# Fifty of 256 gathered dot products move to the matmul engine, and routing is cut into pieces

## The chip, the core and the metric

The kernel runs on one core of a Trainium2 chip. A core has five engines with instruction streams of their own: TensorE (PE) for matmuls, VectorE (DVE), ScalarE (ACT), GpSimd (POOL) and SyncE (SP), which only starts transfers here. Transfers run on 16 DMA engines. The metric is the device time of one execution in microseconds (us).

## What is computed

Two transformer blocks on 256 tokens of width 2048, all in float32. The change is in the last part of the first block, a layer of 16384 small experts ("PEER"). Cut to what matters:

```python
# peer(x = hn, ...): T = 256 tokens, H = 8 heads, K = 16 picks a head, 128 keys a side
qry = (xt @ w_query).reshape(T, H, 2, 128)
s = einsum('thpd,phnd->thpn', qry, sub_keys)          # 2 x 128 scores per token and head
top_s, top_i = top_k(s, 16)                           # the best 16 of each side
cand_s = top_s[:, :, 0, :, None] + top_s[:, :, 1, None, :]
best_s, best_pos = top_k(cand_s.reshape(T, H, 256), 16)
expert_idx = ...                                      # first key * 128 + second key
gates = softmax(best_s)
u = expert_down[expert_idx]                           # one row of 2048 numbers per pick
act = gelu(einsum('td,thkd->thk', xt, u))             # the dot products
y = einsum('thkd,thk->td', expert_up[expert_idx], gates * act)
```

There are 256 x 8 x 16 picks, so 32768 rows of 8 KB of `expert_down` are read, 268 MB.

## The kernel before

**Row tiles.** Tokens stand in two tiles of 128, one token on each of 128 partitions. For tile t, head hd and pick k, one indirect transfer that POOL starts (`gather`, L612) fetches 128 rows, one for each token: a row tile of 128 x 2048, 1.05 MB. There are 2 x 8 x 16 = 256 of them. They are fetched in pairs into a buffer of 16 KB a partition, from a pool of seven such buffers (`bigt`). The pool also holds `h` and `hn` for all this time, `hhi`/`hlo` and `qT` at the start, and a `cchunk` from tile 1 on. So two buffers serve for rows at first, then five, and four in tile 1. A new pair is fetched into a buffer when both row tiles in it have been used.

**The dot product** of a row tile with the tokens is one DVE instruction (L621): it multiplies by `hn[:, t, :]` and sums over 2048 columns into one column of `dots`. After 16 of them ACT takes the Gelu (L625) and DVE multiplies by the gates (L626).

**Routing** (`route`, L564 to L606) finds the 16 picks of one tile and head on DVE: some 30 small instructions, with one Exp on ACT. `route_to` keeps it a head or two ahead of the rows.

**Coefficients.** The sum over `expert_up` is not done row by row for three quarters of the columns, but as a dense product with a matrix of coefficients. It is built per token as an outer product of two one-hot vectors: the second key's one-hot, and the first key's one-hot times the coefficient (L667), by one matmul of 128x128 for each token (L669). A group is four tokens. `store_coefs` builds it for tile 0 while tile 1's rows are fetched, and writes three of four chunks to DRAM (`ct_d`, 2 MB each). `onehots_ahead` has ACT build second-key one-hots for 112 of tile 1's 128 tokens into buffers that are free. What is left for tile 1 (32 groups) comes after the last row tile. Then the products with `expert_up` begin (L807).

**Order.** A scheduler lays out each engine's stream at build time, and each engine then runs its stream strictly in that order, waiting where a semaphore is not there yet. A step of a background generator (`bg`) is taken once a pair of row tiles.

## Time and profile before

| | us |
|---|---|
| median of 3 runs (3211.7 to 3215.2) | 3213.9 |
| the profiled execution | 3219.45 |
| its span from first to last instruction | 3217.7 |
| first gather of a row tile / first gather of head 1 | 827.11 / 886.72 |
| end of the last row tile's dot product | 1573.9 |
| DVE busy / POOL busy / PE busy, whole span | 2535.2 / 879.8 / 2555.4 |

All times in the trace are microseconds from the start of the span. The heads are counted 0 to 15 over both tiles. The stage of the row tiles is from about 827 to 1574, slices 11 to 20 of the page's 40. [...]

### The profile page before, as it was taken

Reading aid. Unit: us, or ns where it says so; the run is one execution under the profiler, and the core shown is the slowest. Engines: PE = TensorE matmul, PEld = TensorE weight load, DVE = VectorE, ACT = ScalarE, POOL = GpSimd, SP = SyncE. Lnnn points to the kernel's source line nnn. Section 1 sums busy time; section 2 is a strip of 40 time slices with the busy share of each in tenths; the row PEclk is TensorE's granted clock in tenths of the full one; section 3 lists DMA queues with packets and bytes.
Section 4 is the critical chain, followed back from the end, with each engine's and each line's share of the span. In section 5 each row is a group of like instructions: output and inputs, shape, how many; then the busy total and the mean of one; then the engine's idle time right before and its main releaser. Section 6 shows DMA issues by size and latency. Waiting matters only on the chain. (4 is left out here: it accounts for less than half of the span.)

```text
span 3217.7 us, 35193 instructions
## 1 busy us (share of the span) xinstructions
PE 2555.4 (79%) x12368; PEld 2141.8 (67%) x12368; DVE 2535.2 (79%) x3682; ACT 1542.9 (48%) x2212; POOL 879.8 (27%) x575
## 2 busy tenths in 40 slices
PE   8999999999910004400399999999999999999999
PEld 7788888888810003300388888889987787878777
DVE  6656544555999999999988888887575799999974
ACT  5534444444310105441244444457445677778764
POOL 0000000000376686667766666620000000000000
PEclk9999999999965555555699999999999999999999
DMA  6455555565899999999789999974654599999964
GB/s 239 151 182 162 184 191 195 187 220 197 328 352 363 331 427 387 376 342 419 285 306 334 335 334 334 334 263 142 204 190 139 201 338 348 381 344 379 348 226 167
DMA packets 302522, 898.22 MB, mean 279 GB/s; under 512 B 20736, under 2 KB 42240, under 8 KB 268288
## 3 DMA queue, kind: packets, MB, share of 16 engines
q1 hardware_dynamic: 226560, 542.88, 48.1%
q0 software_dynamic: 57760, 335.65, 27.3%
q10 hardware_dynamic: 18016, 17.35, 1.6%
q8 instruction: 99, 1.62, 0.2%
q14 instruction: 87, 0.71, 0.1%
HBM read 887.42 MB, written 8.39 MB: 278 GB/s over the span
## 5 line engine op out<-in xcount | busy, mean ns | idle before, releaser
L254 DVE TENSOR_TENSOR wlo<-raw,whi 128x1024 fp32r<-128x1024 f32 (+1 forms) x538 | 648.5, 1208 | 453.1 <-ACT whi L253 446.9
L253 ACT CAST whi<-raw 128x1024 fp32r<-128x1024 f32 (+1 forms) x538 | 559.5, 1041 | 686.9 <-PE pj L284 255.6
L621 DVE CUSTOM_DVE_ANT_0 row<-row,hn 128x2048 f32<-128x2048 f32 x256 | 579.7, 2291 | 6.1 <-DMA row<-in_peer_expert_down_dram,eidx 5.7
L612 POOL DMA_INDIRECT row<-in_peer_expert_down_dram,eidx x256 | 508.4, 1986 | 265.8 <-DVE dots L621 100.7
L199 POOL TENSOR_TENSOR r<-rstdv,mhalf 128x2 f32<-128x2 f32 x5 | 4.5, 890 | 1508.9 <-DVE rstdv L225 1508.9
L612 POOL DMA_INDIRECT urow<-in_peer_expert_up_dram,eidx x256 | 322.8, 1261 | 197.7 <-DVE h L771 143.8
L254 DVE TENSOR_TENSOR wlo<-rawg,whi 128x1024 fp32r<-128x1024 f32 x256 | 313.1, 1225 | 35.1 <-ACT whi L253 10.3
L253 ACT CAST whi<-rawg 128x1024 fp32r<-128x1024 f32 x256 | 270.0, 1056 | 97.9 <-PE pgu L1283 68.6
L282 PE MATMUL pj<-whi,xhi 128*128 128x512 f32 x736 | 289.4, 393 | 1.3 <-ACT whi L253 1.3
L283 PE MATMUL pj<-wlo,xhi 128*128 128x512 f32 x736 | 288.6, 392 | 0.0
L284 PE MATMUL pj<-whi,xlo 128*128 128x512 f32 x736 | 288.2, 392 | 0.0
L639 PE MATMUL pcf<-cc,pk 128*128 128x128 f32 x2 | 0.9, 460 | 340.7 <-DVE pk L626 340.7
L639 PEld LDWEIGHTS pcf<-cc,pk 128*128 128x128 f32 x2 | 0.4, 182 | 341.5 <-issue 177.8
L1282 PE MATMUL pgu<-wlo,xs 128*128 128x512 f32 x512 | 199.8, 390 | 3.1 <-DVE wlo L254 3.1
L1281 PE MATMUL pgu<-whi,xs 128*128 128x512 f32 x512 | 200.0, 391 | 0.0
L1283 PE MATMUL pgu<-whi,xs 128*128 128x512 f32 x512 | 199.2, 389 | 0.0
L771 DVE SCALAR_TENSOR_TENSOR h<-urow,pk,h 128x512 f32<-128x512 f32 x256 | 191.8, 749 | 4.5
L254 DVE TENSOR_TENSOR wlo<-rawd,whi 128x1024 fp32r<-128x1024 f32 x128 | 154.1, 1224 | 12.1 <-ACT whi L253 1.1
L282 PEld LDWEIGHTS pj<-whi,xhi 128*128 128x128 f32 x736 | 138.5, 188 | 29.5 <-ACT whi L253 1.7
L284 PEld LDWEIGHTS pj<-whi,xlo 128*128 128x128 f32 x736 | 138.4, 188 | 28.1
L283 PEld LDWEIGHTS pj<-wlo,xhi 128*128 128x128 f32 x736 | 138.4, 188 | 27.7
L253 ACT CAST whl<-raw 128x1024 fp32r<-128x1024 f32 x96 | 101.2, 1056 | 113.5 <-PE ua L809 83.0
(547 smaller groups left out, 6302.0 us busy)
## 6 DMA issues: line engine op xcount, KB each, us to landing
raw<-in_w_in_dram SPq DMA_DIRECT2D x124, 1024.0 KB
raw<-in_peer_expert_up_dram SPq DMA_DIRECT2D x96, 1024.0 KB
rawg<-in_w_expert_gate_dram SPq DMA_DIRECT2D x128, 512.0 KB
rawg<-in_w_expert_up_dram SPq DMA_DIRECT2D x128, 512.0 KB
rawd<-in_w_expert_down_dram SPq DMA_DIRECT2D x64, 1024.0 KB
raw<-in_w_out_dram SPq DMA_DIRECT2D x32, 1024.0 KB
raw<-in_w_ret_branch_dram SPq DMA_DIRECT2D x16, 1024.0 KB
raw<-in_w_peer_query_dram SPq DMA_DIRECT2D x16, 1024.0 KB
```

What stands on the lines that cost most here:

```text
L199: G.tensor_tensor(out=dst, in0=v, in1=mhalf[:, 0:n], op=ALU.pow)
L253: S.copy(hi, raw)
L254: env["last"] = V.tensor_tensor(out=lo, in0=raw, in1=hi.bitcast(F32), op=ALU.subtract)
L282: TE.matmul(ps[:, t, :], h_, hi, start=st, stop=False)
L283: TE.matmul(ps[:, t, :], h_, lo, start=False, stop=False)
L284: env["mm"] = TE.matmul(ps[:, t, :], l_, hi, start=False, stop=en)
L612: G.indirect_dma_start(out=dst, out_offset=None, in_=src, in_offset=bass.IndirectOffsetOnAxis(ap=idx, axis=0))
L621: V.tensor_tensor_reduce(out=row[:, i, :], in0=row[:, i, :], in1=hn[:, t, :], scale=1.0, scalar=0.0, op0=ALU.mult, op1=ALU.add, accum_out= ...
L771: V.scalar_tensor_tensor(out=h[:, t, 1536:2048], in0=row[:, k, :], scalar=coef[:, t, c0 + k:c0 + k + 1], in1=h[:, t, 1536:2048], op0=ALU.m ...
L1281: TE.matmul(o_, xh, hi[:, :, i, :], start=k == 0, stop=False)
L1282: TE.matmul(o_, xh, lo[:, :, i, :], start=False, stop=False)
L1283: TE.matmul(o_, xl, hi[:, :, i, :], start=False, stop=k == NK - 1)
```

## The change

**Dots on PE.** `PE_DOTS` names the picks whose dot product goes to PE: picks 1, 4, 7, 10 and 13 in heads 1 to 7, picks 3, 7 and 11 in heads 8 to 12, none in heads 0 and 13 to 15. That is 35 + 15 = 50 of 256. For such a row tile PE makes 16 transposes of 128x128, ACT copies them from PSUM in two halves of 1024 columns, and PE makes 16 float32 matmuls against `hT`, the transposed tokens. The diagonal of the 128x128 result holds the dot products, and one DVE instruction over 128 columns multiplies by the identity and sums. `hT` takes one of the seven large buffers from head 1 to head 12.

**Routing in pieces.** `route` yields eight times, and after each pair of row tiles 1.35 pieces are issued. One multiplication of the gates and one negation leave DVE.

**Coefficients.** In tile 0, two of a group's four first-key one-hots come from ACT. For tile 1, first-key one-hots of 64 tokens are built early into a buffer `o1`, which takes a large buffer from head 13 on. There half of the groups need one DVE instruction of 512 columns instead of three of 128 on DVE and one on POOL.

```diff
+PE_DOTS = [()] + [(1, 4, 7, 10, 13)] * 7 + [(3, 7, 11)] * 5 + [()] * 3
+ROUTE = 1.35
...
+    def transposed_copy(dst, src):
+        for g in range(2):
+            ps = acc("pxT")
+            for j in range(8):
+                TE.transpose(ps[:, j // 4, j % 4 * P:(j % 4 + 1) * P], src[:, (g * 8 + j) * P:(g * 8 + j + 1) * P], ident)
+            S.copy(dst[:, g * 8:g * 8 + 8, :], ps.rearrange("p a (b c) -> p (a b) c", b=4))
...
+    def diagonal(ps, dots, k):
+        junk = env["wk"].tile([P, P], F32, tag="dj", name="dj", bufs=1)
+        V.tensor_tensor_reduce(out=junk, in0=ps[:, 0:P], in1=ident, scale=1.0, scalar=0.0,
+                               op0=ALU.mult, op1=ALU.add, accum_out=dots[:, k:k + 1])
...
-                V.tensor_tensor_reduce(out=row[:, i, :], in0=row[:, i, :], in1=hn[:, t, :], scale=1.0, scalar=0.0,
-                                       op0=ALU.mult, op1=ALU.add, accum_out=dots[:, k + i:k + i + 1])
+                if k + i in on_pe:
+                    rT = rTs[step[1] % 2]
+                    step[1] += 1
+                    transposed_copy(rT, row[:, i, :])
+                    ps = pst("pdd")
+                    for d in range(NK):
+                        TE.matmul(ps[:, 0:P], rT[:, d, :], hT[:, d, t * P:(t + 1) * P], start=d == 0, stop=d == NK - 1)
+                    late.append((step[0] + 2, lambda ps=ps, k=k + i: diagonal(ps, dots, k)))
+                else:
+                    env["dot"] = V.tensor_tensor_reduce(
+                        out=row[:, i, :], in0=row[:, i, :], in1=hn[:, t, :], scale=1.0, scalar=0.0,
+                        op0=ALU.mult, op1=ALU.add, accum_out=dots[:, k + i:k + i + 1])
+            settle(step[0])
+            step[0] += 1
+            with tc.issue_after(env["dot"].ins):
+                route_to(16 + int(ROUTE * step[0]))
             yield
...
+            if not oh:
+                onehots(ab4[:, 1, 2:4], kT, c * 32 + q + 2, 2, 0)
+            first = c * 32 + q
+            ahead = o1[0][:, first // 2:first // 2 + 4] if oh and first % 8 == 0 else None
+            if ahead is not None:
+                V.tensor_tensor(out=ab4[:, 1], in0=ahead, in1=cT[:, first:first + 4, None].to_broadcast([P, 4, P]), op=ALU.mult)
             for i in range(4):
...
+                if not oh and i >= 2:
+                    S.mul(ab4[:, 1, i, :], ab4[:, 1, i, :], cT[:, tk:tk + 1])
...
+            if n == 13:
+                pe_done.append(1)
+                o1.append(bigt([P, 64, P], BF16, "o1"))
+            if n == 1:
+                hT = bigt([P, NK, T], name="hT")
+                for t_ in range(2):
+                    transposed_copy(hT[:, :, t_ * P:(t_ + 1) * P], hn[:, t_, :])
+                rTs = [e8([P, NK, P], name="rT"), raw_tile([P, NK, P], "rT")]
```

How the streams change at two places. First DVE in head 1 (a dot product is the pair of rows `row,dots` and `dots`; MAX to MATCH_REPLACE are routing; `nm` is the negation that leaves). Before:

```order
L621 ISA row,dots<-row,hn 128x2048
L621 ISA dots 128x1
L584 MAX_INDEX bp<-bv,rtmp 128x8
L585 MATCH_REPLACE rtmp<-bv,rtmp 128x256
L602 TENSOR_SCALAR nm<-bv 128x1
```

Now, at the same step of routing (`pdd` is PE's result, `dj` a scratch tile):

```order
L592 MAX_INDEX bp<-bv,rtmp 128x8
L668 ISA row,dots<-row,hn 128x2048
L668 ISA dots 128x1
L594 MATCH_REPLACE rtmp<-bv,rtmp 128x256
L642 ISA dj,dots<-pdd,cc 128x128
L642 ISA dots 128x1
L595 MAX bv<-rtmp 128x8
```

The instruction over `pdd` stands between two dot products of rows, one or two dot products behind the pick that it belongs to; DVE waits there until PE has finished that pick.

Second, PE from the end of the query projection on. Before, nothing stands between the scores and tile 0's coefficients:

```order
L677 MATMUL psr<-skT,qT 128x128 x20
L632 MATMUL pky<-cc,pk 128x128 x2
L639 MATMUL pcf<-cc,pk 128x128
L669 MATMUL pcc<-ab_7357 128x128 x4
L669 MATMUL pcc<-ab_7378 128x128 x4
```

Now the picks of heads 1 to 7 stand there, and those of heads 8 to 12 among the coefficient groups:

```order
L736 MATMUL psr<-skT,qT 128x128 x20
L630 MATMUL pxT<-cc,hn 128x128 x19
L630 MATMUL pxT<-cc,row 128x128 x16
L665 MATMUL pdd<-hT,rT 128x128 x16
```

```order
L728 MATMUL pcc<-ab_8910 128x128 x4
L728 MATMUL pcc<-ab_8944 128x128 x4
L630 MATMUL pxT<-cc,row 128x128 x16
L665 MATMUL pdd<-hT,rT 128x128 x16
L728 MATMUL pcc<-ab_9009 128x128 x4
```

PE takes its picks one after another, transposes and matmuls of each before those of the next. POOL still starts the 256 gathers in the same order, but 16 instead of 32 of its multiplications for tile 1 are left.

## Rows read from the trace of the kernel before

**Rows 1.** The page's slices: TensorE's clock, DVE, DMA.
```profile
span 3217.7 us, 35193 instructions
...
DVE  6656544555999999999988888887575799999974
...
PEclk9999999999965555555699999999999999999999
...
```
**Rows 2.** Busy time by stretch: PE, weight loads, DVE, ACT, POOL, clock, DMA share, GB/s.
```profile
887.00:1100.00 213.00, 13.33 (x92) 12.18 (x90) 210.82 (x469) 28.52 (x60) 141.47 (x72) 0.54 0.93 347
1100.00:1204.00 104.00, 0.00 (x0) 0.00 (x0) 103.40 (x101) 1.53 (x4) 85.36 (x44) 0.50 0.99 411
1204.00:1440.00 236.00, 68.51 (x259) 55.73 (x259) 233.68 (x454) 107.01 (x271) 157.99 (x76) 0.53 0.96 367
1440.00:1574.00 134.00, 0.00 (x0) 0.00 (x0) 125.58 (x116) 22.68 (x69) 98.37 (x51) 0.50 0.98 411
...
1500.00:1550.00 50.00, 0.00 (x0) 0.00 (x0) 48.27 (x46) 0.22 (x1) 43.60 (x22) 0.50 1.01 428
```
**Rows 3.** DVE by line, 887 to 1574: count, busy us, mean ns, idle before.
```profile
L621 DVE CUSTOM_DVE_ANT_0 row<-row,hn 128x2048 f32<-128x2048 f32 x242 | 547.7, 2291 | 2.7 <-DMA row<-in_peer_expert_down_dram,eidx 2.3
L667 DVE TENSOR_SCALAR ab<-cc,kT,cT 128x128 f32<-128x128 f32 x128 | 38.6, 372 | 0.0
...
L606 DVE TENSOR_SCALAR pk<-pk,nm 128x16 f32<-128x16 f32 x14 | 4.2, 297 | 0.0
...
L602 DVE TENSOR_SCALAR nm<-bv 128x1 f32<-128x1 f32 x14 | 2.3, 162 | 0.0
...
L641 DVE COPY cT<-pcf 128x128 f32<-128x128 f32 x1 | 0.3, 285 | 0.0
```
**Rows 4.** Who waited for whom, POOL, 887 to 1574: us, times, longest.
```profile
POOL row L612 <- DVE dots L621: 74.0, 25, 6.8
```
**Rows 5.** In order of time, DVE and POOL, four of the rows after 1110.
```profile
1110.80 1.91 POOL L612 DMA_INDIRECT row<-in_peer_expert_down_dram,eidx  x1 [0.30 <-issue]
...
1111.81 2.29 DVE L621 CUSTOM_DVE_ANT_0 row<-row,hn 128x2048 f32<-128x2048 f32 x1
1113.01 1.90 POOL L612 DMA_INDIRECT row<-in_peer_expert_down_dram,eidx  x1 [0.30 <-issue]
...
1114.02 2.29 DVE L621 CUSTOM_DVE_ANT_0 row<-row,hn 128x2048 f32<-128x2048 f32 x1
```
**Rows 6.** In order of time, POOL: head 1's first gather, a run of 31.
```profile
886.72 0.95 POOL L612 DMA_INDIRECT row<-in_peer_expert_down_dram,eidx  x1 [5.17 <-DVE dots L621]
...
898.73 2.41 POOL L612 DMA_INDIRECT row<-in_peer_expert_down_dram,eidx  x1 [0.30 <-issue]
...
980.37 2.82 POOL L612 DMA_INDIRECT row<-in_peer_expert_down_dram,eidx  x1 [0.30 <-DVE bp L587]
```
**Rows 7.** In order of time, PE: 8 transposes at 1.0, float32 matmuls at 0.5 and 1.0.
```profile
783.52 1.04 PE L550 MATMUL psk<-cc,skn 128*128 128x128 f32 x8
...
1216.54 6.80 PE L669 MATMUL pcc<-ab 128*128 128x128 f32 x34 [1.26 <-DVE ab L667]
...
1575.79 27.59 PE L669 MATMUL pcc<-ab,oh 128*128 128x128 f32 x224 [0.85 <-DVE ab L667]
```
**Rows 8.** ACT by line, 1204 to 1440: a one-hot step, a group's copy.
```profile
L648 ACT ACTIVATE ab<-cc,kT 128x128 f32<-128x128 f32 x112 | 36.5, 392 | 38.4 <-DVE pk L598 20.4 <-PE pcc L669 17.4 <-issue 0.4
...
L670 ACT COPY cchunk<-pcc 128x512 f32<-128x512 f32 x32 | 17.7, 586 | 21.1 <-PE pcc L669 21.1
```
**Rows 9.** ACT by line, 700 to 900: one instruction of 1024 columns.
```profile
L253 ACT CAST whi<-raw 128x1024 fp32r<-128x1024 f32 x59 | 62.0, 1053 | 99.9 <-PE pq L294 42.2 <-PE pwo L284 42.0 <-DMA raw<-in_w_peer_query_dram 11.1
```
**Rows 10.** In order of time: the last dot product, tile 1's coefficients, the first product.
```profile
1571.65 2.29 DVE L621 CUSTOM_DVE_ANT_0 row<-row,hn 128x2048 f32<-128x2048 f32 x1
...
1575.30 4.04 DVE L667 TENSOR_SCALAR ab<-cc,kT,cT 128x128 f32<-128x128 f32 x15
...
1610.43 0.48 PE L807 MATMUL ua<-whi,chi 128*128 128x512 f32 x1
```

## Prediction, made before the changed kernel was run

> **What bounds the kernel now.** I read the slices first, to find where the change works. From slice 11 to 20 DVE stands at 9 tenths, and from slice 12 TensorE's clock at 5 or 6: this is the stage of the row tiles, and only there is PE idle and DVE full [rows 1]. Then the busy times by stretch. From 887 to 1440 DVE is busy for 548 of 553 us; PE has 0 to 29% [rows 2]. In DVE's groups the dot products stand first with 2.29 us each, and DVE sat idle before them for 2.7 us in all, always for a transfer [rows 3]. On the other side POOL waited 74.0 us for dot products to give back a buffer [rows 4]. So DVE is the bound over most of the stage. One thing in the same view speaks against a simple sum, though: from 1100 to 1204 and from 1440 to 1574, where there is hardly any routing, the transfers run at 411 GB/s at a DMA share of 0.98 or 0.99, and at 428 with 1.01 from 1500 to 1550 [rows 2]. A row tile is 128 x 8 KB = 1.049 MB, at 428 GB/s 2.45 us; dot products follow each other in 2.21 us (1111.81, 1114.02) [rows 5]. There the transfers are already slower than DVE, and DVE only lives on tiles that had come before. What DVE is given back can be used only as far as row tiles can come faster.

> **What DVE saves.** Fifty dot products go: 50 x 2.21 = 110 us. Fifty instructions over 128 columns of PSUM come. The trace has none; the nearest rows are a copy of 128x128 out of PSUM at 0.285 and a multiply with two scalars over 128 columns at 0.372 [rows 3]. With its read of the sum I take 0.35, so 17 us (14 to 23). Per route the negation and the gates' multiplication leave: 14 x (0.162 + 0.297) = 6 us [rows 3]. Half of tile 0's 128 first-key one-hots leave: 64 x 0.27 = 17 us, by 4.04 us for 15 in a row [rows 10]. Together 110 - 17 + 6 + 17 = 116 us less work on DVE.

> **What the transfers allow.** From the first gather of head 1 at 886.72 [rows 6] to the last tile's landing at about 1571.65 [rows 10] are 685 us for 240 row tiles, 251.7 MB, and 6.3 MB of coefficients that go to DRAM. At 428 GB/s [rows 2] that is 603 us. So at most 82 of the 116 can be had.

> From this I take off:
> - *The start of head 1, 9 us.* Its first pair now goes into a buffer of the query projection, since `hT` takes the one that it had. Before, POOL ran without a wait from 898.73 on [rows 6], 12 us after 886.72, when the projection's buffers had come free. I take 9; the bounds are 0 and 12.
> - *DVE still full in heads 8 to 10, 4 us.* From 887 to 1574 DVE was busy for 674 us [rows 2]; less 242 x 2.21 and 128 x 0.27 leaves 104 for 14 routes, 7.4 each. With 1.35 pieces of an eighth for each pair a head has 10 us of routing. Heads 8 to 10 then hold 13 x 2.21 + 3 x 0.35 + 16 x 0.27 + 10 = 44 us of DVE against 39 to 43 of transfers.
> - *Coupling, 25 us.* Transfers run at 428 only with a queue in front of them. The stretches that they bound had 411 with their ends [rows 2]; 258 MB at 411 is 628 us, 25 more. Bounds: 0, and 100 at the 367 GB/s of 1204 to 1440, where however DVE was the bound. I stay with 411, since here too the transfers are the bound. Rows now have four buffers instead of five in heads 1 to 7, and three instead of four for most of heads 8 to 15.

> 82 - 9 - 4 - 25 = 44 us.

> **What hides the rest.** PE: 8 transposes take 1.04 us at the full clock, and 224 records of float32 matmuls 27.59 us. These were 28 groups of four, so two records a matmul: 0.25 us at the full clock, 0.40 at half (34 records in 6.80) [rows 7]. A pick is 2.1 + 3.9 = 6 us of PE at the full clock, and about 3.2 + 6.4 = 9.6 at half, with 1.05 us for each half's copy on ACT [rows 9], of which one is behind the transposes. Heads 1 to 7 need 5 picks in 39 us: 30 us at the full clock, 48 at half. At half clock PE would be busy without a pause; the run of 27.59 us, which had none, went at the full clock's 0.25 a matmul though the stretch before it had 0.50 [rows 2, 7]. So I expect it to alternate and the picks to take 7 to 8 us on average, within the 7.8 that there are. ACT: 10 copies of 1.05 a head are little in heads 1 to 7. In tile 0's coefficients it was busy for 107 of 236 us [rows 2], about 2.4 for each group, and gets two more one-hot steps, a shorter second step and two multiplications, 4 x 0.3 + 0.3 = 1.5 us (a step of 128 columns is busy 0.39 and a copy of 512 0.59 [rows 8]; in a run they overlap). With 8 groups and 6 copies a head that is 38 of 43 us, close. Their cover is the 1.35 us a pair by which transfers are late; if it is gone, heads 8 to 12 lose what the third rival counts.

> **After the rows.** Tile 1's coefficients run at PE's pace: 27.59 us for 28 groups, out of 36.6 from the last dot product to the first product [rows 7, 10]. DVE and POOL get less there, PE the same. I take 0 (0 to 3 us less).

> **Sum.** The profiled execution is 3219.45, 5.5 above the median; the stage is in both, so I take the 44 (rounded to 43) from the median: 3213.9 - 43 = 3171 us. The ends for this case: 82 - 0 + 3 = 85 less at best; at worst 82 - 12 - 8 - 40 = 22 less. So 3129 to 3192.

> **The rivals.**
> 1. *The diagonals hold up DVE; slower.* DVE runs in order, and the instruction on PE's result stands one or two dot products behind its pick. Behind it stand the next dot products, for which POOL's next gathers wait. In a saturated stream PE's result is there 7 to 11 us after the tile landed; DVE is there after 4.7 (one dot product) or 7.2 (two). If DVE lags its tiles by 4 us, as four buffers of 4.9 us a pair permit, the wait is gone; with three it need not be. DVE has 116 us of slack against the old time, 2.3 us for each of 50 waits; from there on the kernel is slower. At 3.0 us on average, PE mostly at half clock: 685 - 116 + 150 = 719, 34 more, 3248. For it: PE at 0.53 in the stretch where it worked with pauses [rows 2]. Against: five picks at half clock leave no pause.
> 2. *POOL cannot start gathers faster; no change.* A gather under a running dot product ends 0.9 us after that dot product's end (1110.80 + 1.91 against 1111.81) [rows 5], while one with DVE free takes 0.95 [rows 6]. From 898.73 to 980.37 POOL started 31 gathers without waiting for a buffer, 2.72 us apart [rows 6]. At that pace 240 take 653, with the stores 15 and the start 9 more, 677: 8 less, 3206. For it: dots and routing mixed, as they stay. Against: 11 instead of 16 dot products a head stand in the way. [...]
> 3. *Heads 8 to 12 gain nothing.* ACT at 38 of 43 us, PE in order behind coefficients that wait for ACT and DVE, three buffers: their five heads stay at what they had, and about 23 of the 44 are lost: 3193.
> 4. *The stream sinks to what mixed stretches had.* With PE, ACT and DVE all at SBUF the tiles come at 360 GB/s (347 to 367 [rows 2]): 258 MB in 717, with the start 726, 41 more, 3255. Against: POOL waited for buffers there [rows 4], so the rate was DVE's. [...]

> **How the numbers follow.** Forecast 0.60; rival 1 0.13; rival 2 0.12; rival 3 0.12; rival 4 0.03. A measurement of this kernel tells some 0.2% from no change, 6.4 us. Faster: forecast, rival 3 and half of rival 2, 0.78. Same: half of rival 2 and 0.02 of rival 1, 0.08. Slower: the rest, 0.14. The range takes the forecast's own down to 3138, rivals 2 and 3 and the mild end of rival 1: 3138 to 3222.

> **What would show it.** Right: from head 1 on, DVE idle before dot products for transfers (tens of us instead of 2.7), DMA at 400 GB/s or more from 900 to 1500, the last dot product at about 1530, 50 instructions on `pdd` at about 0.35 with little idle time before them, PE partly at 1.0 in heads 1 to 7. Heads 13 to 15, which were bound by transfers already, should be 2 to 3 us longer each, not shorter. Wrong: a large idle time of DVE before `pdd` (rival 1), POOL without a pause at 2.7 a gather (rival 2), heads 8 to 12 at 50 us each (rival 3), a DMA share near 1 at 360 GB/s (rival 4).

## The result, and the profile after

The changed kernel takes 3254.1 us (median of four runs, 3250.3 to 3260.6), the kernel before 3214.6 on the same chip. The ratio is 1.0126 (95% interval 1.0108 to 1.0145): slower by 1.3%, clear of the noise, where 3171 was forecast.

The slices of the changed kernel first, beside those of [rows 1]:

```profile
span 3248.5 us, 40431 instructions
...
DVE  6656544455999987768988888888575789999974
...
PEclk9999999999999987775699999999999999999999
...
DMA  6454555565899997899699999974654599999964
```

DVE is no longer at 9 tenths from slice 15 on, and the granted clock (PEclk, in tenths of full speed) is up in the first half of the stage. But its span is 30.8 us longer, and a table of where it went reads unlike anything in the prediction. All times are starts of gathers and of the first product in each trace; e9, e5 and e10 are kernels of the experiments below.

| us | before | changed | e9 | e5 | e10 |
|---|---|---|---|---|---|
| start to the first gather | 827.1 | 844.7 | 827.2 | 826.8 | 828.3 |
| head 0 | 59.6 | 62.4 | 64.0 | 64.3 | 61.8 |
| heads 1 to 7 | 306.9 | 276.2 | 276.7 | 276.1 | 295.5 |
| heads 8 to 11 | 209.8 | 234.0 | 237.3 | 204.2 | 181.1 |
| heads 12 to 15, to the last gather | 154.7 | 160.2 | 161.0 | 161.4 | 161.7 |
| from there to the first product | 52.3 | 44.9 | 44.6 | 44.5 | 44.3 |
| first product to the end | 1607.3 | 1626.1 | 1600.6 | 1601.0 | 1599.3 |
| median of the runs | 3214.6 | 3254.1 | 3212.9 | 3180.1 | 3175.2 |

So two things went wrong. The first gather comes 17.6 us late and the part behind the stage takes 18.8 more, in code that the change does not touch. And the stage itself gained 30.7 in heads 1 to 7 and gave 24.2 of it back in heads 8 to 11.

**Outside the stage.** Two stretches in which PE is busy without a pause, of the kernel before (columns as in [rows 2], the counts of matmuls in brackets behind PE):

```profile
500.00:680.00 180.00, 180.00 (x804) 149.16 (x803) 89.70 (x76) 76.72 (x80) 0.00 (x0) 1.00 0.61 204
1700.00:1900.00 200.00, 200.00 (x884) 165.67 (x883) 173.05 (x245) 95.55 (x148) 122.55 (x98) 1.00 0.97 336
```

The same of the changed kernel, ahead of them its row stage:

```profile
950.00:1150.00 200.00, 153.60 (x1190) 145.12 (x1191) 178.27 (x388) 64.37 (x85) 128.77 (x81) 0.92 1.01 426
...
1200.00:1420.00 220.00, 125.51 (x784) 119.39 (x785) 157.45 (x306) 147.52 (x382) 89.62 (x60) 0.74 0.80 309
1420.00:1588.00 168.00, 28.94 (x200) 27.71 (x198) 146.21 (x142) 87.02 (x245) 113.16 (x63) 0.60 0.98 403
...
500.00:680.00 180.00, 180.00 (x785) 146.16 (x784) 88.51 (x76) 73.94 (x76) 0.00 (x0) 1.00 0.59 198
1700.00:1900.00 200.00, 200.00 (x862) 162.15 (x861) 171.07 (x240) 92.98 (x146) 109.09 (x96) 1.00 0.93 327
```

PE is full at clock 1.00 in both, and from 1700 to 1900 does 884 matmuls in the one and 862 in the other: 2.5% fewer. Each float32 operand of these products is split into two float32r parts, `..hi` and `..lo`. From start to start, matmuls of 512 columns are 226.7 ns apart in the kernel before (the 576 for `pb`, which run without a pause: each 226 or 227). In the changed kernel they are 232.4 apart on average (the 2304 for `ua` and `ub`, from 228 to 241), from the first ones on and with nearly all operands; only two groups of the second block stay at 227 (median), the 768 for `oa` and the 48 for `pu`. Other engines' instructions take what they took (ACT's casts of 1024 columns, `whi<-raw`, 1054 ns before and 1049 now, DVE's `wlo` 1223 in both). Before the stage there are 2208 matmuls for `pj`, 576 for `pb` and 384 for `pwo`: 3168 x 5.73 ns = 18.2 us, against the 17.6 that the first gather is late. The expert_up stage has 2304, so 13.2 us, and the 1151 for `pqk`, `pwo` and `pgt` behind it make 6.6 more, against 18.8.

**In the stage.** In the windows above heads 1 to 7 (950 to 1150) run at 426 GB/s and a DMA share of 1.01, as forecast; from 1200 to 1420 it is 309 at 0.80, with no engine full. DVE's groups of the changed kernel, 907 to 1588 (against [rows 3]), and POOL's longest wait for DVE there (against [rows 4]):

```profile
L668 DVE CUSTOM_DVE_ANT_0 row<-row,hn 128x2048 f32<-128x2048 f32 x192 | 436.1, 2287 | 34.7 <-DMA row<-in_peer_expert_down_dram,eidx 30.2 <-issue 3.6
L726 DVE TENSOR_SCALAR ab<-cc,kT,cT 128x128 f32<-128x128 f32 x64 | 19.9, 346 | 8.4 <-PE pcc L728 8.4
...
L642 DVE CUSTOM_DVE_ANT_0 dj<-pdd,cc 128x128 f32<-128x128 f32 x50 | 14.3, 287 | 68.6 <-PE pdd L665 65.6 <-issue 3.0
```
```profile
POOL row L623 <- DVE dots L668: 53.7, 18, 9.6
```

DVE now waits for transfers before dot products (34.7 us instead of 2.7), and 65.6 before the 50 instructions on PE's result. In heads 1 to 7 (907 to 1183) it worked for 247.1 of 276 us and waited for both of these, more for PE than for transfers:

```profile
907.00:1183.00 276.00, 213.59 (x1668) 201.66 (x1669) 247.12 (x536) 96.68 (x127) 181.85 (x112) 0.93 1.00 419
...
DVE dj L642 <- PE pdd L665: 16.3, 13, 3.7
DVE row L668 <- DMA row<-in_peer_expert_down_dram,eidx: 7.0, 11, 1.5
```

Who waited for whom from 1183 to 1417, heads 8 to 11, shows a ring, in which each engine waits for the next:

```profile
PE pdd L665 <- ACT rT L631: 53.8, 9, 10.1
ACT cchunk L729 <- PE pcc L728: 45.4, 17, 6.4
DVE dj L642 <- PE pdd L665: 39.5, 9, 8.5
...
PE pcc L728 <- DVE ab L726: 20.3, 2, 10.3
PE pxT L630 <- DMA row<-in_peer_expert_down_dram,eidx: 17.8, 5, 5.3
```

One turn of it, in order of time, PE, ACT, DVE and POOL of the changed kernel:

```profile
1279.69 2.73 PE L630 MATMUL pxT<-cc,row 128*128 128x128 f32 x12
1279.84 0.39 ACT L698 ACTIVATE ab<-cc,kT 128x128 f32<-128x128 f32 x1
...
1281.70 0.98 ACT L698 ACTIVATE ab<-cc,kT 128x128 f32<-128x128 f32 x3
1282.57 0.62 ACT L699 ACTIVATE ab<-ab 128x512 f32<-128x512 f32 x1
...
1283.95 1.28 ACT L615 ACT_TABLE_LOAD   x1
...
1286.13 1.90 ACT L631 COPY rT<-pxT 128x1024 f32<-128x1024 f32 x2
1286.81 2.29 DVE L668 CUSTOM_DVE_ANT_0 row<-row,hn 128x2048 f32<-128x2048 f32 x1 [7.13 <-DMA row<-in_peer_expert_down_dram,eidx]
...
1287.18 6.36 PE L665 MATMUL pdd<-hT,rT 128*128 128x128 f32 x32 [4.76 <-ACT rT L631]
1287.89 2.03 POOL L623 DMA_INDIRECT row<-in_peer_expert_down_dram,eidx  x1 [12.38 <-ACT rT L631]
...
1293.38 1.95 PE L728 MATMUL pcc<-ab 128*128 128x128 f32 x16
1293.58 0.29 DVE L642 CUSTOM_DVE_ANT_0 dj<-pdd,cc 128x128 f32<-128x128 f32 x1 [1.89 <-PE pdd L665]
...
1294.47 0.58 ACT L729 COPY cchunk<-pcc 128x512 f32<-128x512 f32 x1 [6.44 <-PE pdd L665]
```

The pick's transposes end at 1282.4, but on ACT one-hots of later coefficient groups and a table load stand ahead of its copies, until 1286.13. PE stands still meanwhile, comes back mostly at half the full clock (granted 0.50 from 1287.2 to 1292.5, then 1.00; 6.36 us for 32 records), and the next groups' matmuls wait behind it; then ACT waits 6.44 for PE. DVE and POOL are held in the same turn.

### The profile page after: what moved, and what is told of

Read it like the earlier page. It is cut to its first block, busy times and chain, and to the rows that moved or that the text cites. A ratio compares the mean times of both kernels' runs of the same rounds, so it can differ in the third digit from the quotient of the medians.

```text
span 3248.5 us, 40431 instructions
## 1 busy us (share of the span) xinstructions
PE 2896.3 (89%) x14800; PEld 2439.0 (75%) x14800; DVE 2432.1 (75%) x3554; ACT 1716.9 (53%) x2576; POOL 752.4 (23%) x559
## 5 line engine op out<-in xcount | busy, mean ns | idle before, releaser
L623 POOL DMA_INDIRECT row<-in_peer_expert_down_dram,eidx x256 | 419.9, 1640 | 356.2 <-issue 89.0
L668 DVE CUSTOM_DVE_ANT_0 row<-row,hn 128x2048 f32<-128x2048 f32 x206 | 468.0, 2286 | 35.8 <-DMA row<-in_peer_expert_down_dram,eidx 31.3
L623 POOL DMA_INDIRECT urow<-in_peer_expert_up_dram,eidx x256 | 297.7, 1163 | 230.0 <-DVE h L859 166.1
L257 DVE TENSOR_TENSOR wlo<-rawg,whi 128x1024 fp32r<-128x1024 f32 x256 | 313.1, 1225 | 41.9 <-ACT whi L256 37.2
L665 PE MATMUL pdd<-hT,rT 128*128 128x128 f32 x1600 | 223.9, 307 | 90.1 <-ACT rT L631 88.9
L665 PEld LDWEIGHTS pdd<-hT,rT 128*128 128x128 f32 x1600 | 215.7, 220 | 101.0 <-ACT rT L631 98.8
L630 PE MATMUL pxT<-cc,row 128*128 128x128 f32 x800 | 114.6, 305 | 61.7 <-DMA row<-in_peer_expert_down_dram,eidx 60.8
```

The costliest lines, as they stand in the source:

```text
L257: env["last"] = V.tensor_tensor(out=lo, in0=raw, in1=hi.bitcast(F32), op=ALU.subtract)
L623: G.indirect_dma_start(out=dst, out_offset=None, in_=src, in_offset=bass.IndirectOffsetOnAxis(ap=idx, axis=0))
L665: TE.matmul(ps[:, 0:P], rT[:, d, :], hT[:, d, t * P:(t + 1) * P], start=d == 0, stop=d == NK - 1)
L668: env["dot"] = V.tensor_tensor_reduce(out=row[:, i, :], in0=row[:, i, :], in1=hn[:, t, :], scale=1.0, scalar=0.0, op0=ALU.mult, op1=ALU.ad ...
```

## The experiments

**e1: the addresses.** The change makes an unused tile `pad` 16 instead of 8 numbers wide (two buffers, 64 bytes), `dots` has three buffers instead of two (64 bytes), and a new `rgate` takes 128 bytes in the stage's own pool; the diff ahead of the prediction does not show these lines. All buffers behind the small-tile pool thus lie 128 bytes higher, while the large buffers below it stay.

```diff
-    sm.tile([P, 16], F32, tag="pad", name="pad")
```

> The changed kernel without its unused tile `pad` in the small-tile pool: every buffer behind that pool (raw weights, whi, wlo, all phase buffers) then lies 128 bytes lower, at the addresses of the kernel before; nothing else changes. Theory A (the addresses slow TensorE's 512-column matmuls, which took 232.4 ns instead of 226.7 from start to start in every stage of the kernel, the untouched ones too): pitch back to 226.7, head 0 starts at 827 instead of 845, the stages outside the row tiles lose 36 us, and only the row stage's own gain of about 6 is left: 3206 to 3212. Rival (the pitch belongs to the chip or the execution, or to a longer program, not to addresses): pitch stays at 232.4, 3250 to 3258. Rival 2 (buffers of the row stage matter too): between, with the first head at 827 but the row stage changed by more than 5 us.

Measured: 3228.8 us, ratio to before 1.0041 (1.0027 to 1.0054). Its two stretches:

```profile
500.00:680.00 180.00, 180.00 (x804) 149.19 (x803) 89.55 (x76) 76.85 (x80) 0.00 (x0) 1.00 0.60 204
1700.00:1900.00 200.00, 200.00 (x858) 160.86 (x858) 170.61 (x235) 92.29 (x145) 115.58 (x97) 1.00 0.93 324
```

The first is back at 804, and the first gather at 827.0. The expert_up stage is not (858, a pitch of 233.3 ns). So addresses it is, since an unused tile is all that differs; but my number was 17 too low even at its upper end, because one stage had kept the slow pitch.

**e2: 64 bytes in the kernel before.**

```diff
-    sm.tile([P, 8], F32, tag="pad", name="pad")
+    sm.tile([P, 16], F32, tag="pad", name="pad")
```

> The kernel before with its unused tile `pad` twice as large: the buffers behind the small-tile pool move up by 64 bytes, nothing else changes. Theory A, if a multiple of 256 bytes is what the wide matmuls want: pitch 230 to 233, 3240 to 3255. Theory A, if only the changed kernel's odd multiple of 128 hurts: 3214. Rival (no address matters): 226.7 and 3214.

Measured: 3224.1, ratio 1.0029 (1.0017 to 1.0040), so a kernel whose program is otherwise the same gets 10 us slower. My size, 3240 or more, was a miss. Again the two stretches tell more than the sum:

```profile
500.00:680.00 180.00, 180.00 (x796) 147.88 (x796) 88.62 (x76) 76.26 (x79) 0.00 (x0) 1.00 0.61 203
1700.00:1900.00 200.00, 200.00 (x884) 165.68 (x883) 174.73 (x246) 95.69 (x149) 124.59 (x99) 1.00 0.96 333
```

796 (228.9 ns) in the first, 884 (226.7) in the second, which is untouched although both its operands moved by 64. With the addresses of the built programs that gives one rule for these runs: the pitch goes with the distance of the two operands, taken mod 256. `whi` streams; `xhi` (or `mhi`, `rhi`) and, in expert_up, `chi` are loaded as weights. For `chi` the table has the lowest of the four buffers that `chi` and `clo` share; the others lie multiples of 4096 above it:

```
            whi     xhi     chi     (whi-xhi) mod 256  pitch   (whi-chi) mod 256  pitch, expert_up
before      165632  121344  203520          0          226.7           0               226.7
e2          165696  121344  203584         64          228.9           0               226.7
changed     165760  121344  203776        128          232.4         128               232.4
e1          165632  121344  203648          0          226.7         128               233.3
e3, e4      165632  121344  203648          0          226.7         128               232.4
e5, e9      165632  121344  203776          0          226.7           0               226.7
```

The group `oa`, which kept its pace in the changed kernel, fits the rule: both its operands had moved by 128 there (`whi` at 165760, the weights `hhl` at 192384), and their distance is a multiple of 256.

**e3: no picks in heads 8 to 12.**

```diff
-PE_DOTS = [()] + [(1, 4, 7, 10, 13)] * 7 + [(3, 7, 11)] * 5 + [()] * 3
+PE_DOTS = [()] + [(1, 4, 7, 10, 13)] * 7 + [()] * 8
```

> As e1, and heads 8 to 12 without dot products on TensorE (35 instead of 50). Theory B (in heads 8 to 11, which took 58 us each against 52 before, PE, ACT and DVE wait for each other in turn around each of the three picks, and none is full): DVE then has 16 dot products, about 8 us of routing and 4 us of coefficients a head, 48 to 50 us, so heads 8 to 11 fall from 58 to 48 to 50 each, 32 to 40 us less than e1: 3166 to 3180. Rival (ACT's longer coefficient groups, two more first-key one-hots each, hold the heads whatever the picks do): heads stay at 56 to 58, 3200 to 3212.

Measured: 3192.7, ratio 0.9927 (0.9911 to 0.9942). It is 36.1 less than e1, within the 32 to 40 expected. Heads 8 to 11 take 53.3, 50.0, 51.6 and 49.6. DVE is full again in heads 9 and 10 (1225 to 1325 of e3); in head 8 it was busy for 44.0 of 53 us:

```profile
1225.00:1275.00 50.00, 16.71 (x56) 12.91 (x56) 49.59 (x92) 32.61 (x94) 27.02 (x17) 0.50 0.87 331
1275.00:1325.00 50.00, 21.67 (x73) 16.69 (x73) 49.93 (x96) 35.14 (x100) 28.73 (x16) 0.50 0.92 375
```

**e4: less on ACT instead.** As e1, all of tile 0's first keys on DVE:

```diff
-            if not oh:
-                onehots(ab4[:, 1, 2:4], kT, c * 32 + q + 2, 2, 0)
```

> As e1, with tile 0's first-key one-hots all on VectorE as in the kernel before, so ACT has four steps of 128 columns less in a group (2 squares and 2 products) and one of 256 less. Theory B (the picks in order): ACT's queue before a pick's copy is shorter by a quarter to a third, so heads 8 to 11 gain only part, 54 to 56 each: about 3198 to 3206. Rival (ACT's groups hold the heads): 48 to 50 each, 3170 to 3180. If DVE is what decides: 4 to 5 us longer each, 3225.

Measured: 3198.0, ratio 0.9946 (0.9931 to 0.9961). Heads 8 to 11 take 52 each, between both expectations. All picks are still there, but PE's nine waits for `rT` fall from 58.4 us (e9, heads 8 to 11, the first row) to 17.2 (e4):

```profile
PE pdd L664 <- ACT rT L630: 58.4, 9, 10.1
...
PE pdd L664 <- ACT rT L630: 17.2, 9, 4.1
```

So neither the picks nor ACT's longer groups do it alone: it is the picks' copies standing behind those groups.

**e5: both distances right.** As e3, with `rgate` of 256 bytes:

```diff
-    rgate = env["wk"].tile([P, 32], F32, tag="rg", name="rgate", bufs=1)
+    rgate = env["wk"].tile([P, 64], F32, tag="rg", name="rgate", bufs=1)
```

> As e3, and `rgate` 64 instead of 32 numbers wide (the second half unused): the pool behind it, which holds the coefficients `chi` and `clo` that TensorE loads as weights in the expert_up stage, lies 128 bytes higher again. In e1, e3 and e4 that stage alone kept a pitch of 232.4 to 233.3 ns, and there the weights alone had moved; in e2 both operands had moved by 64 there and the pitch was 226.7, while in the other stages only the streamed operand had moved and it was 228.9. Theory A2 (what counts is the distance between the addresses of the loaded weights and of the streamed operand, which is best at a multiple of 256 bytes): 226.7 in every stage, the time from the first expert_up product to the end back from 1611 to 1607 us as before: 3186 to 3191. Rival (the absolute address of the weights counts, and 203520 was a good one): 230 to 234 in that stage, 3190 to 3196.

Measured: 3180.1, ratio 0.9896 (0.9879 to 0.9912), 12.6 below e3, and 226.7 ns in every stage. `chi` now lies 256 bytes above its old place and loses nothing, so the absolute address is not what counts.

**e6: three buffers, no picks in heads 8 to 11.**

```diff
-PE_DOTS = [()] + [(1, 4, 7, 10, 13)] * 7 + [()] * 8
+PE_DOTS = [()] + [(1, 4, 7, 10, 13)] * 7 + [()] * 4 + [(15,)] + [()] * 3
```

> As e5, with one dot product on TensorE again, the last of head 12: `hT` then keeps its buffer through heads 8 to 12, and these have three buffers for row tiles as in the changed kernel, but no picks in heads 8 to 11. Theory B (the picks in order between coefficient groups made these heads long): they stay at 50 to 53, as in e3: 3186 to 3198. Rival C (the third buffer that `hT` took made them long, not the picks): 56 to 60, 3215 to 3230.

Measured: 3189.6, ratio 0.9917 (0.9900 to 0.9933). Heads 9 to 11 stay at 51.0, 51.5 and 49.5, so the missing buffer does not hold them; head 8 alone takes 60.0 instead of 52.9. Theory B stands. Whether those 7 us are the buffer's is not shown: head 8 of e8 below takes 58.2 with four buffers.

**e7: routing earlier.**

```diff
-ROUTE = 1.35
+ROUTE = 1.75
```

> As e5, with the routing taken at 1.75 instead of 1.35 pieces a pair, so it is done by the end of head 7 instead of the middle of head 10. Theory D (in heads 8 to 10 VectorE is now the bound: 16 dot products 35.4, first keys 4.3, routing 10 of 50 us; in heads 1 to 7 it has slack against the transfers): heads 8 to 10 fall from 52 to 43 to 46, heads 1 to 7 stay at 39 to 41: 3162 to 3175. Rival (ACT and PE with the coefficient groups hold heads 8 to 11, as head 11 without routing took 49.6): heads 8 to 10 fall by 0 to 3 each, 3180 to 3191. If heads 1 to 7 have no slack: they take 43 each and it comes out even, 3186.

Measured: 3181.4, ratio 0.9894 (0.9877 to 0.9910), as e5. Heads 8 to 10 fall to 47.4, 47.7 and 40.8, but heads 1 to 7 take 43.8 on average: there was no slack for it. From 950 to 1150 DVE worked for 177.4 us and waited for PE's results for 20.8, together 198 of 200. The expectation of e10 below calls it full; it was not full of work, but the diagonals' waits had taken its slack:

```profile
950.00:1150.00 200.00, 144.01 (x1104) 138.54 (x1104) 177.36 (x421) 61.09 (x85) 106.90 (x73) 0.85 0.98 385
...
DVE dj L641 <- PE pdd L664: 20.8, 11, 4.3
```

**e8: no dot products on PE.** As e5, with `PE_DOTS = [()] * 16`.

> As e5, with no dot product on TensorE at all; the routing in pieces and tile 0's first keys half on ScalarE stay. The transposed copy of the tokens is still made once, and its buffer comes free for row tiles. Theory (the 35 picks in heads 1 to 7 gave the 31 us of those heads): heads 1 to 7 at 42 to 46 each, VectorE 35.4 + 10 = 45 us: 3215 to 3235, slower than e5 by 30 to 45. Rival (what those heads gained came from routing in pieces, which no longer holds up gathers): 40 each, 3188 to 3200.

Measured: 3216.8, ratio 1.0006 (0.9996 to 1.0015). The 35 picks in heads 1 to 7 are worth 36.8 us, the buffer that `hT` takes for them already taken off; the rest of the change without them brings nothing that can be told. From 950 to 1150 of e8 DVE is full and the transfers are at 383 GB/s:

```profile
950.00:1150.00 200.00, 0.69 (x2) 0.29 (x2) 198.25 (x339) 14.40 (x29) 119.70 (x71) 0.50 0.98 383
```

**e9: the whole change, both distances right** (the edits of e1 and e5 in the changed kernel).

> The whole change with both distances right: without the unused `pad` and with `rgate` 64 wide, as in e5, and with all 50 dot products on TensorE. Theory A2: 226.7 ns in every stage; against e1 the expert_up stage gives back what e5 gave back against e3, 12.6 us by the medians: about 3216, and so 36 to 40 less than the changed kernel; what is left of the change is then no difference, since the 31 us that heads 1 to 7 gain go into heads 8 to 11 (58 each instead of 52) and 12 to 15. Rival (the row stage itself also suffered from the addresses): 3195 to 3205.

Measured: 3212.9, ratio 0.9995 (0.9986 to 1.0004): no difference from before, and 41.2 us less than the changed kernel. That is what the 128 bytes cost.

**e10: a sixth pick, and routing earlier.** As e5, with:

```diff
+PE_DOTS = [()] + [(1, 4, 6, 9, 12, 14)] * 7 + [()] * 8
+ROUTE = 1.75
```

> As e5, with six instead of five dot products a head on TensorE in heads 1 to 7 and the routing at 1.75 pieces a pair. Theory D (in e7 VectorE was full in heads 1 to 7, with 13 instead of 10 us of routing; a sixth pick takes 1.9 of it away): heads 1 to 7 at 40 to 42, heads 8 to 10 at 45 to 47 as in e7: 3163 to 3173. Rival (TensorE, 6 to 7 us a pick in order, has no room for a sixth in 40 us, and VectorE waits for it): heads 1 to 7 at 44 to 47, 3182 to 3200.

Measured: 3175.2, ratio 0.9876 (0.9861 to 0.9891), the best of all; 2 us over what was expected. Heads 1 to 7 take 42.2 on average and heads 8 to 11 45.3, where e7 has 43.8 and 44.9.

**e11: `ROUTE = 1.5`,** otherwise e5.

> As e5, with the routing at 1.5 pieces a pair, between e5 (1.35) and e7 (1.75), which came out alike. If routing is only moved between two stretches that VectorE bounds: 3178 to 3183, as both. If heads 1 to 7 have slack up to some rate below 1.75: heads 1 to 7 stay at 40, heads 8 to 10 fall by 2 to 4 each, 3168 to 3176.

Measured: 3184.2, ratio 0.9904 (0.9889 to 0.9919), 1 us above the first expectation: alike, so routing is only moved between two stretches that have no slack.

**e12: the same picks, the coefficient groups later.** As e9, with:

```diff
-                if n == 8 and j == 2:
+                if n == 13 and j == 2:
...
-                if next(bg, 1) and t and n > 8 and kT1 is None:
+                if next(bg, 1) and t and n > 13 and kT1 is None:
```

> As e9, with the three picks a head in heads 8 to 12, but tile 0's coefficient groups begin in head 13 instead of head 8, two for each pair of rows; tile 1's one-hots then come mostly after the rows, so the whole kernel must be longer, and heads 8 to 12 are what is read. Theory B (picks and coefficient groups wait for each other in the order of PE, ACT and DVE): without the groups heads 9 to 12 take 39 to 43 each, as the transfers allow. Rival (three picks a head with three buffers are slow by themselves): 50 to 58 each.

Measured once: 3222.8. Heads 8 to 12 take 40.0, 43.0, 47.5, 37.1 and 37.3, on average 41.0 where e9 has 56.1; head 10 is above what was expected. The stretch in e12 and then in e9:

```profile
1167.00:1375.00 208.00, 112.57 (x751) 107.85 (x751) 179.52 (x298) 41.52 (x55) 145.75 (x81) 0.76 0.99 400
```
```profile
1168.00:1405.00 237.00, 132.27 (x840) 126.26 (x839) 167.15 (x330) 149.99 (x386) 98.32 (x64) 0.75 0.79 310
```

With three picks a head the transfers run at 400 GB/s once ACT has no groups (41.5 us busy instead of 150). The heads after them pay for it, 50 to 53 each. But e12 does not test the rival as it was put: `cchunk` takes its large buffer only when the groups begin, so the rows had four buffers in heads 8 to 12 of e12, and three in e9. What speaks against the rival is head 12 of the changed kernel, with three picks, three buffers and 5 groups instead of 8. It took 40.0 us, and transfers ran at 410 GB/s:

```profile
1417.00:1457.00 40.00, 25.46 (x187) 24.42 (x185) 30.60 (x37) 24.67 (x62) 24.80 (x16) 0.85 1.00 410
```

How much of the 59 us that e9 takes in heads 8 to 11 a fourth buffer alone would give back, with picks and groups both there, was not run.

## Why the prediction was wrong

- **The step that failed first is the sum itself:** "the stage is in both, so I take the 44 from the median". It took everything outside the row stage as unchanged. The change moved addresses, and e9 shows 41.2 us for that. No rival held this; that rival 1's 3248 is near the measured time is luck, since its reason was another. That is half of the 83 us between forecast and result. The other half is in the stage: with the addresses right it gives 1.7 us (e9), no difference that can be told, instead of 43.
- **The term that failed next is what hides the rest in heads 8 to 12.** I put ACT at 38 of 43 us a head, "close", and its cover as the 1.35 us a pair by which transfers are late. The size of the sum was right (in e9 150 us of ACT over heads 8 to 11, 37.5 each); what it left out is the order. Busy shares were no measure: from 1200 to 1420 ACT was busy for 148 of 220 us, PE for 126, DVE for 157, and they waited for each other in order. Rival 3 had the place and the parts right, but priced it as "gain nothing". Heads 8 to 11 in fact lost 27.5 us against before (237.3 in e9 against 209.8). By e12, though with a fourth buffer, and by head 12 of the changed kernel the picks need the groups for it; by e3 and e6 the groups need the picks. e4 shows the link between them, the picks' copies behind the groups on ACT.
- **Heads 1 to 7 were right:** 426 GB/s, 39.5 us a head, PE at clock 0.92 and some 6 us a pick (153.6 us of 950 to 1150, in which about 25 picks fall) instead of 7 to 8. By e8 the dot products on PE bring 36.8. But transfers were not the only bound there: DVE worked for 247.1 us of 276 and waited 16.3 for PE's results and 7.0 for row tiles, so it had no slack either, which e7 and e11 then showed.
- **Rates.** The coupling of 25 us was spread evenly in my sum. In heads 1 to 7 there was none, and all of it and more fell in heads 8 to 11, at 309 GB/s. Rival 2 is refuted: gathers started fast enough for 426. Rival 4 named a low rate as its own cause; here the low rate is the ring's effect, since the same three picks a head go with 400 GB/s in e12 and 410 in head 12 of the changed kernel.
- **Diagonals.** 0.287 us instead of 0.35 each, and 65.6 us of waiting where little was forecast, 1.3 for each of 50, under the 2.3 at which rival 1 put the turn. Most of it (39.5) is in the ring.
- **Small terms.** Head 0 took 4.4 longer with the addresses right (e9), where I had 9 for the start of head 1. Heads 13 to 15 took 1.5 longer each in e9 (117.6 against 113.1) and 2.4 in the changed kernel (120.2), in the direction expected. From the last dot product to the first product it took 34.0 us instead of 36.5, within the 0 to 3 that I had; the 7.4 in the table count from the last gather.
- **What would show it.** 426 GB/s and a clock of 0.92 (950 to 1150) came as said. Idle DVE before dot products came too, but of its 34.7 us only 7 are in heads 1 to 7. The last dot product at 1588 instead of 1530, and heads 8 to 11 at 58, were the signs of rival 3 and worse.

By place, e9 against before: head 0 +4.4, heads 1 to 7 -30.2, heads 8 to 11 +27.5, heads 12 to 15 +6.3, to the first product -7.7: +0.3 in the stage. Behind it e9 is 6.7 shorter. The profiled execution of before was 5.5 over its median, so that may be the execution's; it is not shown.

What stays open: why a distance of 128 costs 5.7 ns a matmul, why e1 has 233.3 where e3 and e4 have 232.4 at the same addresses, and what a distance of 192 costs, which was not tried.

## What to carry to other kernels

When a change adds or widens any small tile, compare the addresses of the large ones: an added 128 bytes cost here more than 35 saved dot products gave (41.2 us against 36.8), and it shows as fewer matmuls in a stretch where PE is full in both profiles (785 against 804 from 500 to 680). Work put on an idle engine must be seen in that engine's order: from 1183 to 1417 of the changed kernel ACT was busy for only 150.2 of 234 us, and PE waited 53.8 us for its copies and DVE 39.5 for PE, since the piece that they needed stood behind work that nobody needed yet. When an experiment takes such work away, see what else it gives back: here it also freed a buffer. So put such pieces where no other generator feeds the same queues (heads 1 to 7 here), and leave the rest.
